# Two attentions on one Trainium2 core: a third buffer for transposed weights, halved GpSimd passes, a second raw weight slot

## The chip, the cores and the metric

The kernel runs on one core of a Trainium2 chip. The metric is the device time of one execution in microseconds. Three runs of the kernel before took 3191.88, 3189.90 and 3182.48 us (median 3189.9).

## What is computed

Two blocks follow each other on one sequence of 1024 tokens with 1024 channels, in float32. The first has a gated chunk mixer and an attention over 16 heads of 64 channels; the second has a state-space mixer, a per-layer embedding, a second attention of the "stick-breaking" kind, and another embedding. The two attentions, cut to what matters here:

```
# first attention (three dilations, here one table of added penalties)
q, k, v = heads(h @ w_in)                 # 16 heads x 1024 x 64
p = softmax(q k^T / 8 + alibi, causal)    # rows of weights, 128 at a time
y = (p v) * silu(h @ w_gate)
...
# second attention
q, k, v = norm(u @ s_in), norm(h @ w_kv), h @ w_kv'
z = q k^T;  w = sigmoid(z) * running product of sigmoid(-z) from the right
y = ((w v) * silu(gate)) @ w_out
```

Each matrix of weights is scaled by a row of gains where the reference has a norm in front of it, as in all projections of the second attention.

## The kernel before

Nothing here is scheduled by hand on the chip. The builder holds generators ("streams") with priorities and runs them against a small model of the engines (`Sched`, L207 on): whichever stream of highest priority is ready by the model emits its next instructions. What comes out is one fixed order for each engine, and each engine works through its own order and waits on semaphores. So a change of a buffer count changes the order in which everything near it is emitted.

Products are made in float32r as three matmuls, hi x hi, hi x lo and lo x hi. A weight block of 128x1024 elements is loaded from memory into a raw slot (`Weights.loads`, L384), multiplied on POOL (GpSimd) by its gain if it has one, copied as hi by ACT and subtracted as lo by POOL (`Weights.splits`, L397), which puts hi and lo into a split slot. There are two split slots in the attentions (`limit`, L434). Raw slots lie at 0, 4 and 208 KB of each partition; the first attention uses all three, the second only the one at 0, since 4 KB is used for other tiles there.

An attention goes over 8 pairs of heads. For each pair, `project_pair` makes v, q, k and the gate (12 or 24 matmuls of 512 columns in a row; low priority, so it fills what the attention leaves). The scores stream (`sstream`, L1403 and L2010) makes rows of scores: two matmuls of up to 512 columns for each PSUM bank of three (two in the first attention), then DVE, ACT and, in the second attention, a DVE scan (L2058) and a POOL product (through L521) turn a row into weights. `weigh` (L1283) has two streams on top: `xs` (L1292) transposes weights on PE in groups of up to four 128x128 blocks into one of two PSUM banks, ACT writes hi and DVE writes lo into a buffer of the resource `pt2`, and `vs` (L1321) multiplies that buffer with v, four matmuls a group, and releases it. `pt2` has two buffers of 4 KB, at 164 and 168 KB (L1390, L1997). There are 160 such groups in each attention. v of a pair lies in one of two slots, so v of pair p+1 can only be projected when the products of pair p-1 are done.

Names in the rows: psum<-ident,m172f is a transpose of weights; psum<-m156r,m140r or psum<-m156r with 256 columns or less is the product with v; psum<-m108r followed by psum<-m140r,m108r or m200r,m108r are scores; psum<-m44r,m8r and the like (m44r, m60r, m76r, m92r with m8r, m16r) are projections. L536 is every matmul, L547 every transpose, L521 every two-input POOL operation, L502 and L507 DVE, L498 most of ACT. After the second attention `stick_out` (L2161) multiplies its result, which goes through memory and POOL (`load_halves`, L2213), with the last projection matrix.

Of the kernel before, what the change touches and what calls it, by code (L numbers as in the profile page):

```python
# [15 lines left out]
ALU = mybir.AluOpType  # L16
# [6 lines left out]
P = 128  # L23
# [9 lines left out]
def R(ap):  # L33
    return ap.bitcast(F32R)
# [7 lines left out]
class Tok:  # L42


    def __init__(self, t=None):
        self.t = t
# [23 lines left out]
class Arena:  # L70


    CUTS = (0, 8, 16, 24, 40, 44, 60, 76, 92, 108, 140, 156, 172, 192, 200, 208, 216)

    def __init__(self, pool):
        self.pool = pool
        self.kb = [0.0] * self.CUTS[-1]
        self.blocks = [Block(a, b - a) for a, b in zip(self.CUTS, self.CUTS[1:])]
        self.of = [x for x in self.blocks for _ in range(x.n)]
# [286 lines left out]
class Weights:  # L366
# [30 lines left out]
    def splits(self):  # L397
        b = self.b
        for g in self.list:
            yield (g.loaded, self.split)  # L400
            g.out = self.split.get()
            n = g.nk * g.nc
            hi = g.out[:, :n].rearrange("p (k c) -> p k c", k=g.nk)
            lo = g.out[:, KB4:KB4 + n].rearrange("p (k c) -> p k c", k=g.nk)
            dep = g.loaded.t
            if g.gain is not None and g.nk <= 2:

                yield (dep, b.s.FA)
                for k in range(g.nk):
                    e = b.A(R(hi[:, k, :]), g.rawv[:, k, :], AF.Copy, dep, scale=g.gain[:, k:k + 1])  # L410
                for k in range(g.nk):
                    yield (e, b.s.FV)
                    t = b.Vstt(R(lo[:, k, :]), g.rawv[:, k, :], g.gain[:, k:k + 1], hi[:, k, :], ALU.mult, ALU.subtract, e)
                self.raw.put(g.slot, t)
                g.hi, g.lo = R(hi), R(lo)
                g.ready.t = t
                yield 0.0
                continue
            if g.gain is not None:
                yield b.s.FG  # L420
                dep = b.Gtt(g.rawv, g.rawv, g.gain.unsqueeze(2).to_broadcast([P, g.nk, g.nc]), ALU.mult, dep)
            if b.hi_on_pool:
                dep = b.Gts(R(hi), g.rawv, 1.0, 0.0, ALU.mult, ALU.add, dep)
            else:
                yield (dep, b.s.FA)
                dep = b.A(R(hi), g.rawv, AF.Copy, dep)
            yield (dep, b.s.FG)
            t = b.Gtt(R(lo), g.rawv, hi, ALU.subtract, dep)
            self.raw.put(g.slot, t)
            g.hi, g.lo = R(hi), R(lo)  # L430
            g.ready.t = t
            yield 0.0

    def limit(self, n, m=3):  # L434

        self.split.slots, self.raw.slots = self.all[:n], self.all_raw[:m]
# [5 lines left out]
class Builder:  # L442
    def __init__(self, ctx, tc, a, out=None):
        self.ctx, self.tc, self.nc, self.a, self.out = ctx, tc, tc.nc, a, out
        self.s = Sched()
        self.hi_on_pool = False
        nc = self.nc
        pool = lambda n, **k: ctx.enter_context(tc.tile_pool(name=n, bufs=1, **k))
        cp = pool("const")
        self.dram = pool("dram", space=DRAM)  # L450
        self.ident = cp.tile([P, P], F32, name="ident")
        make_identity(nc, self.ident)
        self.mhalf = cp.tile([P, 8], F32, name="mhalf")
        nc.gpsimd.memset(self.mhalf, -0.5)
        self.cols = cp.tile([P, 256], F32, name="cols")
        self.smallt = cp.tile([P, 256], F32, name="smalls")
        self.mask = cp.tile([P, P], F32, name="mask")
        nc.gpsimd.memset(self.mask, 0.0)
        nc.gpsimd.affine_select(self.mask, self.mask, pattern=[[-1, P]], compare_op=ALU.is_gt, fill=-1e30, base=0,
                                channel_multiplier=1)  # L460
        self.zero = cp.tile([P, 1], F32, name="zero")
        nc.gpsimd.memset(self.zero, 0.0)
        self.nsmall = 0
        self.rq = cp.tile([P, 96], F32, name="rq")
        self.ps = pool("psum", space=PSUM).tile([P, 8, 512], F32, name="psum")
        self.arena = Arena(pool("arena"))
        self.bank = [Bank(self.ps[:, i, :]) for i in range(8)]
        self.pg, self.pt, self.px, self.pv = [Res([]) for _ in range(4)]
# [574 lines left out]

    def merge(self):
        self.banks("012", "3", "456", "7")

        a, s = self.a, self.s
        gl, ml, ls = self.res(172, 4, 2), self.res(180, 4, 2), self.res(188, 4, 3)
# [43 lines left out]
        g = gr.get().rearrange("p (a c) -> p a c", a=2)  # L1092
# [289 lines left out]
    def attention1(self):  # L1382
# [4 lines left out]
        self.att_tok = self.halves()  # L1387
        self.stack_pools()
        pr = Ring(self, 172, 20)
        pt2, ops = self.res(164, 4, 2, "r"), self.res(192, 1, 2)  # L1390
        tmp, Ts = Res([self.region(o, 2) for o in (40, 42, 194, 196, 198)]), self.res(24, 4, 2)
        self.W.limit(2)
        self.new_pairs()

        T = {(p, h): Tok() for p in range(8) for h in range(2)}
# [593 lines left out]
    def stick(self):  # L1989
# [4 lines left out]
        self.stk_tok, self.sgd_tok = self.halves(), [Tok() for _ in range(8)]  # L1994
        self.stack_pools()
        pr, tr_ = Ring(self, 172, 20), Ring(self, 24, 16)
        pt2, ops = self.res(164, 4, 2, "r"), self.res(192, 1, 2)  # L1997
        tmp = Res([self.region(o, 2) for o in (4, 6, 40, 42, 194, 196, 198)])
        self.W.limit(2, 1)
        self.tail_slots, self.all_scored = tmp, Tok()  # L2000
        gains = self.smallt[:, 252:254]
        for o in (0, 64):
            e = self.dma(gains[o:o + 64, 0:1], a["q_norm_2"].rearrange("o d -> d o"))
            e = self.dma(gains[o:o + 64, 1:2], a["k_norm_2"].unsqueeze(1))
# [156 lines left out]
    def stick_out(self):  # L2161
        self.banks("012", "34", "567", "7")
        a, s = self.a, self.s
        act = self.act1
        W = self.W
        act.tt = self.next_tt

        def more():
            yield self.all_scored
            self.hi_on_pool = False  # L2170
            W.raw.slots = W.all_raw
            W.split.slots = W.all[:4] + [self.region(o, 8, "r") for o in (140, 148)]

        s.spawn(1, more())
        self.hq = self.scratch("hq", [S, D])
        ev0, begin0, hq_tok = self.partial(self.hq, self.tail_slots)

        turn = [Tok() for _ in range(NT)]

        def begin_turn(cb, t):  # L2180
            yield from begin0(cb, t)
            n = cb * NT + t - self.TURN[0]
            if n % self.TURN[1] == 0 and 0 <= n // self.TURN[1] < NT:
                turn[n // self.TURN[1]].t = s.now

        hd1 = [(self.all_scored, t, n) for t, n in zip(self.hd1_tok, turn)]
        hq_go = [(self.all_scored, t) for t in hq_tok]
        h, he, ha, hr = self.residual(self.res(108, 4, NT).slots, [(self.hd1, hd1), (self.hq, hq_go)], self.res(180, 4, 2))
        yield from self.gemm_a(act, self.J["so", 0], ev0, begin=begin_turn)
        nj, es, half = self.res(172, 4, 2), Res([self.region(o, 2) for o in (188, 190, 212, 214)]), {}  # L2190
        pact = self.embed(1, 156, self.res(188, 1, 4), self.weighed)

        def ev(cb, t, ps, e):
            sl = slice(cb * 512, cb * 512 + 512)
            return self.Vtt(h[t][:, sl], h[t][:, sl], ps, ALU.add, max(e, he[t].t))

        def fin(t, e):
            act.tt[0][t], act.tt[1][t] = Tok(), Tok()
            s.spawn(1, self.raw_tile(act, h[t], t, (e, ha[t]), nj, half))

        def begin(cb, t):
            yield he[t]

        yield from self.gemm_a(act, self.J["so", 1], ev, fin, 4, begin, (5, 6, 7))
        W.split.slots = W.split.slots + W.all[4:]

        def store(t, e):
            yield e
            self.dma(self.out[0, t * P:(t + 1) * P, :], h[t], e)

        yield from self.ple(1, act, pact, h, half, es, lambda t, e: s.spawn(1, store(t, e)))
# [70 lines left out]
```

## Time and profile before

| what | value |
|---|---|
| profiled execution | 3192.31 us, of which the span is 3190.6 us |
| median of three runs | 3189.9 us |
| TensorE busy | 3066.8 us, 96% of the span |
| VectorE, ScalarE, GpSimd busy | 1694.9, 1410.7 and 1104.3 us |
| mean granted TensorE clock | 0.978 of full speed |
| first attention | about 450 to 1040 us |
| second attention | about 2340 to 3020 us |

The time around the span is 1.7 us. TensorE (PE) is the engine with work nearly all the time, so the places to look at are those where it sits idle or where its granted clock falls below 1.00. The rows come from a view of busy time by stretches, from timelines of one engine, and from a table of who waited for whom.

### The profile page before, as it was taken

How to read it: one execution, taken by the hardware profiler on the slowest of the kernel's cores; microseconds unless marked ns; L12 is line 12 of the kernel's file. 1: busy time of each engine (PE TensorE's matmuls, PEld its weight loads, DVE VectorE, ACT ScalarE, POOL GpSimd, SP SyncE). 2: the span in 40 equal slices, each digit the busy share in tenths (PEclk: the TensorE clock that was granted, in tenths of full speed). 3: DMA queues.
4: the chain of work that ended last, by engine and by line, in shares of the span. 5: the costliest groups of instructions: out<-in, count | busy, mean ns of one | idle time of the engine just before them, and what ended most of it. 6: DMA issues, size and time to landing. Idle time of an engine off the chain costs nothing. (4 is left out here: it accounts for less than half of the span.)

```text
span 3190.6 us, 40526 instructions
## 1 busy us (share of the span) xinstructions
PE 3066.8 (96%) x15374; PEld 2557.1 (80%) x15374; DVE 1694.9 (53%) x3008; ACT 1410.7 (44%) x2511; POOL 1104.3 (35%) x694
## 2 busy tenths in 40 slices
PE   7999999999999999999999999999999999998899
PEld 6888888888888788888787877778887878887787
DVE  2111146666664422447676666463447777877552
ACT  4322145555564311324242424232457776776431
POOL 3323211111111333324455542401336655668510
PEclk9999999999999999999999999999999999999999
DMA  4112221221212754232333344470201111113621
GB/s 140 58 62 76 96 64 45 63 62 58 60 54 73 253 184 171 92 96 69 89 110 94 108 95 144 135 251 27 93 16 34 40 40 40 40 41 118 220 83 53
DMA packets 270551, 290.87 MB, mean 91 GB/s; under 512 B 14660, under 2 KB 202228, under 8 KB 270356
## 3 DMA queue, kind: packets, MB, share of 16 engines
q1 hardware_dynamic: 270356, 288.29, 28.9%
q8 instruction: 120, 1.97, 0.3%
q14 instruction: 75, 0.61, 0.1%
HBM read 216.80 MB, written 71.43 MB: 90 GB/s over the span
## 5 line engine op out<-in xcount | busy, mean ns | idle before, releaser
L502 DVE TENSOR_TENSOR m156r<-psum,m156r 128x384 fp32r<-128x384 f32 (+2 forms) x376 | 223.9, 605 | 147.6 <-ACT m156r L498 145.3
L498 ACT ACTIVATE m156r<-psum 128x384 fp32r<-128x384 f32 (+2 forms) x376 | 196.7, 535 | 185.6 <-PE psum L547 176.4
L521 POOL TENSOR_TENSOR m172f<-m172f,m24f 128x127 f32<-128x127 f32 (+7 forms) x128 | 181.0, 1424 | 156.2 <-DVE m24f L2058 108.2
L2058 DVE TENSOR_TENSOR_SCAN m24f<-m24f,zero 128x128 f32<-128x128 f32 (+7 forms) x128 | 219.4, 1722 | 6.5 <-ACT m24f L498 5.5
L547 PE MATMUL psum<-ident,m172f 128*128 128x128 f32 (+1 forms) x1314 | 206.5, 281 | 15.5 <-DVE m172f L507 7.2
L521 POOL TENSOR_TENSOR m16r<-m0f,m16r 128x1024 fp32r<-128x1024 f32 (+1 forms) x44 | 107.9, 2452 | 301.1 <-ACT m16r L498 250.3
L498 ACT ACTIVATE m192f<-psum 64x256 f32<-64x256 f32 (+2 forms) x230 | 102.1, 445 | 239.7 <-PE psum L536 137.7
L521 POOL TENSOR_TENSOR m8r<-m0f,m8r 128x1024 fp32r<-128x1024 f32 x42 | 102.7, 2445 | 274.9 <-ACT m8r L498 237.1
L547 PEld LDWEIGHTS psum<-ident,m172f 128*128 128x128 f32 (+1 forms) x1314 | 158.9, 144 | 43.8 <-DVE m172f L507 9.0
L521 POOL TENSOR_TENSOR smalls<-smalls,mhalf 128x1 f32<-128x1 f32 (+1 forms) x104 | 92.1, 886 | 278.4 <-DVE smalls L509 277.7
L536 PE MATMUL psum<-m108r 128*128 128x512 f32 (+3 forms) x384 | 143.2, 375 | 13.0 <-ACT m172f L498 11.3
L536 PE MATMUL psum<-m200r,m108r 128*128 128x512 f32 (+1 forms) x480 | 151.0, 395 | 0.0
L513 DVE SCALAR_TENSOR_TENSOR m172f<-m172f,psum 128x512 f32<-128x512 f32 x64 | 43.7, 686 | 188.9 <-ACT m172f L498 144.1
L1427 DVE CUSTOM_DVE_ANT_0 m172f<-psum,m24f 128x512 f32<-128x512 f32 (+1 forms) x192 | 102.8, 553 | 65.0 <-PE psum L536 64.8
L1435 ACT ACTIVATE m172f<-m172f,smalls 128x128 f32<-128x128 f32 (+7 forms) x128 | 99.3, 776 | 82.9 <-DVE smalls L509 81.2
L536 PE MATMUL psum<-m44r,m8r 128*128 128x512 f32 x504 | 134.6, 405 | 1.1 <-DVE m108r L513 1.1
L507 DVE TENSOR_SCALAR m172f<-m172f,smalls 128x512 f32<-128x512 f32 (+7 forms) x160 | 122.6, 766 | 24.3 <-POOL smalls L521 19.8
L536 PE MATMUL psum<-m60r,m8r 128*128 128x512 f32 x504 | 133.3, 398 | 0.3
L536 PE MATMUL psum<-m76r,m8r 128*128 128x512 f32 x504 | 132.3, 397 | 0.0
L536 PE MATMUL psum<-m60r,m16r 128*128 128x512 f32 x492 | 132.2, 399 | 0.0
L536 PE MATMUL psum<-m92r,m8r 128*128 128x512 f32 x504 | 130.7, 395 | 0.0
L536 PE MATMUL psum<-m44r,m16r 128*128 128x512 f32 x492 | 130.6, 402 | 0.0
(425 smaller groups left out, 7647.2 us busy)
## 6 DMA issues: line engine op xcount, KB each, us to landing
m0f<-in_w_in_dram SPq DMA_DIRECT2D x48, 512.0 KB, 3.8
m0f<-in_m_in_dram SPq DMA_DIRECT2D x26, 512.0 KB, 4.1
m208f<-in_w_in_dram SPq DMA_DIRECT2D x24, 512.0 KB, 3.8
m92f<-acum SPq DMA_DIRECT2D x21, 512.0 KB, 9.4
m24f<-in_alibi_dram SPq DMA_DIRECT2D x16, 512.0 KB, 4.6
m172f<-zd SPq DMA_DIRECT2D x32, 256.0 KB, 10.2
yd<-m172f SPq DMA_DIRECT2D x32, 256.0 KB, 2.3
m108f<-hd SPq DMA_DIRECT2D x16, 512.0 KB, 8.4
```

The lines of the kernel that those rows point to most:

```text
L498: self.nc.scalar.activation(out, in_, func, **k)
L502: self.nc.vector.tensor_tensor(out, a, b, op=op)
L507: self.nc.vector.tensor_scalar(out, a, s1, None, op0=op0)
L513: self.nc.vector.scalar_tensor_tensor(out, a, s, b, op0=op0, op1=op1)
L521: self.nc.gpsimd.tensor_tensor(out, a, b, op=op)
L536: self.nc.tensor.matmul(out, l, r, start=start, stop=stop)
L547: self.nc.tensor.transpose(out, in_, self.ident[:in_.shape[0], :in_.shape[0]])
L1427: nc.vector.tensor_tensor_reduce(row[:, k0:k0 + w], bank[:, :w], Tt[:, off + k0:off + k0 + w], 1.0, -3e38, op0=ALU.add, op1=ALU.max, accum ...
L1435: nc.scalar.activation(row[:, :n], row[:, :n], AF.Exp, bias=nm, accum_out=l)
L2058: nc.vector.tensor_tensor_scan(x[:, ::-1], x[:, ::-1], self.zero.to_broadcast([P, n]), 1.0, op0=ALU.mult, op1=ALU.add)
```

## The change

It does three things. `pt2` gets a third buffer of 4 KB at 212 KB in both attentions; for that the block of 8 KB at 208 is cut into two. While `short` is set, which is during the first attention and in the second up to the end of its scores, POOL's gain pass and its lo pass over a weight block of 128x1024 become two of 128x512 each. And the second attention has raw slots at 0 and 208 KB in place of the one at 0.

```diff
-    CUTS = (0, 8, 16, 24, 40, 44, 60, 76, 92, 108, 140, 156, 172, 192, 200, 208, 216)
+    CUTS = (0, 8, 16, 24, 40, 44, 60, 76, 92, 108, 140, 156, 172, 192, 200, 208, 212, 216)
...
             if g.gain is not None:
                 yield b.s.FG
-                dep = b.Gtt(g.rawv, g.rawv, g.gain.unsqueeze(2).to_broadcast([P, g.nk, g.nc]), ALU.mult, dep)
+                for ks in self.pieces(g):
+                    e = b.Gtt(g.rawv[:, ks, :], g.rawv[:, ks, :], g.gain[:, ks].unsqueeze(2).to_broadcast(
+                        [P, ks.stop - ks.start, g.nc]), ALU.mult, dep)
+                    yield b.s.FG
+                dep = e
...
-            t = b.Gtt(R(lo), g.rawv, hi, ALU.subtract, dep)
+            for ks in self.pieces(g):
+                t = b.Gtt(R(lo[:, ks, :]), g.rawv[:, ks, :], hi[:, ks, :], ALU.subtract, dep)
+                yield b.s.FG
...
+    def pieces(self, g):
+
+        n = g.nk // 2 if self.b.short and g.nk > 1 else g.nk
+        return [slice(k, min(k + n, g.nk)) for k in range(0, g.nk, n)]
...
-        pt2, ops = self.res(164, 4, 2, "r"), self.res(192, 1, 2)
+        pt2, ops = Res([self.region(o, 4, "r") for o in (164, 168, 212)]), self.res(192, 1, 2)
...
-        self.W.limit(2, 1)
+        self.W.limit(2)
+        self.W.raw.slots = [self.W.all_raw[0], self.W.all_raw[2]]
+        self.short = True
...
         def more():
             yield self.all_scored
+            self.short = False
```

The number of matmuls and transposes is the same, 14956. By kind of work the order on PE is the same outside the two attentions; what moves in the other stages is which PSUM bank or slot is taken. Of the 160 groups of transposed weights in each attention, 54 now go into the buffer at 212 KB (m212r). In POOL's order 88 passes are in halves, 30 in the first attention and 58 in the second, and the two halves always follow each other directly.

**First attention, PE, where pair 0 ends and pair 1 begins** (the row ahead of both pieces is the 256-column scores of pair 1; L536 and L547 are L547 and L558 in the changed file). Before:

```order
L536 MATMUL psum<-m92r,m8r 128x512 x3
L536 MATMUL psum<-m108r 128x384
L536 MATMUL psum<-m140r,m108r 128x384
L536 MATMUL psum<-m108r 128x512
L536 MATMUL psum<-m140r,m108r 128x512
L536 MATMUL psum<-m156r,m140r 128x256 x4
L547 MATMUL psum<-ident,m172f 128x128 x3
L536 MATMUL psum<-m156r,m140r 128x256 x4
L547 MATMUL psum<-ident,m172f 128x128 x3
L536 MATMUL psum<-m156r,m140r 128x256 x2
L536 MATMUL psum<-m156r,m140r 128x128 x2
L547 MATMUL psum<-ident,m172f 128x128 x4
```

Now:

```order
L547 MATMUL psum<-m92r,m8r 128x512 x3
L547 MATMUL psum<-m108r 128x384
L547 MATMUL psum<-m140r,m108r 128x384
L547 MATMUL psum<-m92r,m8r 128x512 x3
L547 MATMUL psum<-m156r,m140r 128x256 x4
L547 MATMUL psum<-m108r 128x512
L547 MATMUL psum<-m140r,m108r 128x512
L547 MATMUL psum<-m212r,m140r 128x256 x4
L547 MATMUL psum<-m156r,m140r 128x256 x2
L547 MATMUL psum<-m156r,m140r 128x128 x2
L547 MATMUL psum<-m44r,m16r 128x512 x9
L558 MATMUL psum<-ident,m172f 128x128 x3
```

Pair 0's last groups were transposed earlier, one of them into m212r, so their products stand together, and nine projection matmuls now stand between them and pair 1's first transposes.

**Second attention, PE, where pair 4 ends**, from one point of the work on. Before:

```order
L547 MATMUL psum<-ident,m172f 128x128 x4
L536 MATMUL psum<-m156r,m140r 128x256 x4
L547 MATMUL psum<-ident,m172f 128x128 x3
L536 MATMUL psum<-m108r 128x128
L536 MATMUL psum<-m140r,m108r 128x128
L536 MATMUL psum<-m108r 128x256
L536 MATMUL psum<-m140r,m108r 128x256
L536 MATMUL psum<-m156r,m140r 128x256 x6
L536 MATMUL psum<-m156r,m140r 128x128 x2
L547 MATMUL psum<-ident,m172f 128x128 x4
L536 MATMUL psum<-m108r 128x384
L536 MATMUL psum<-m140r,m108r 128x384
```

Now:

```order
L547 MATMUL psum<-m212r,m140r 128x256 x2
L547 MATMUL psum<-m212r,m140r 128x128 x2
L547 MATMUL psum<-m108r 128x128
L547 MATMUL psum<-m140r,m108r 128x128
L547 MATMUL psum<-m108r 128x256
L547 MATMUL psum<-m140r,m108r 128x256
L547 MATMUL psum<-m108r 128x384
L547 MATMUL psum<-m140r,m108r 128x384
L547 MATMUL psum<-m108r 128x512
L547 MATMUL psum<-m140r,m108r 128x512
L558 MATMUL psum<-ident,m172f 128x128 x8
L547 MATMUL psum<-m108r 128x512
```

The scores of four rows now stand back to back, where transposes and products stood between them.

**End of the second attention, PE** (m140r,m76r is the first product of the last projection that needs the last heads' results). Before:

```order
L536 MATMUL psum<-m156r 128x256 x8
L547 MATMUL psum<-ident,m172f 128x128 x3
L536 MATMUL psum<-m156r 128x256 x2
L536 MATMUL psum<-m156r 128x128 x2
L536 MATMUL psum<-m140r,m76r 128x512 x30
L547 MATMUL psum<-ident,m172f 128x128 x4
```

Now:

```order
L547 MATMUL psum<-m16r,m44r 128x512 x3
L547 MATMUL psum<-m212r,m156r 128x256 x2
L547 MATMUL psum<-m212r,m156r 128x128 x2
L547 MATMUL psum<-m16r,m44r 128x512 x3
L547 MATMUL psum<-m8r,m60r 128x512 x6
L547 MATMUL psum<-m16r,m60r 128x512 x6
L547 MATMUL psum<-m8r,m60r 128x512 x6
L547 MATMUL psum<-m16r,m60r 128x512 x6
L547 MATMUL psum<-m8r,m60r 128x512 x6
L547 MATMUL psum<-m16r,m60r 128x512 x6
L547 MATMUL psum<-m8r,m60r 128x512 x6
L547 MATMUL psum<-m16r,m60r 128x512 x6
L547 MATMUL psum<-m140r,m76r 128x512 x48
```

The last product with v now has 51 projection matmuls behind it before m140r,m76r begins, where it stood in the midst of those.

## Rows read from the trace of the kernel before

**Rows 1.** Profile page, part 1, and busy time of the two attention stages (us, each engine's busy us, PEclk, DMA share).

```profile
PE 3066.8 (96%) x15374; PEld 2557.1 (80%) x15374; DVE 1694.9 (53%) x3008; ACT 1410.7 (44%) x2511; POOL 1104.3 (35%) x694
...
455.00:1030.00 575.00, 563.58 (x3099) 485.33 (x3097) 376.66 (x1041) 331.55 (x664) 77.12 (x32) 0.99 0.20 60
2340.00:2960.00 620.00, 585.08 (x3170) 492.37 (x3169) 468.78 (x650) 432.80 (x821) 378.07 (x227) 0.96 0.16 47
```

**Rows 2.** Busy time in three stretches of the first attention, same columns.

```profile
500.00:520.00 20.00, 16.43 (x93) 13.60 (x93) 14.38 (x34) 13.02 (x28) 2.34 (x1) 0.83 0.14 37
660.00:680.00 20.00, 16.75 (x78) 14.09 (x77) 12.40 (x34) 10.78 (x21) 2.26 (x1) 0.83 0.14 39
800.00:820.00 20.00, 16.74 (x99) 14.57 (x98) 13.81 (x36) 13.00 (x28) 2.36 (x1) 0.91 0.13 37
```

**Rows 3.** PE timeline of the first attention (start, us, instruction, idle before).

```profile
513.22 0.41 PE L547 MATMUL psum<-ident,m172f 128*128 128x128 f32 x1 [2.09 <-DVE m172f L507]
514.53 0.69 PE L547 MATMUL psum<-ident,m172f 128*128 128x128 f32 x2 [0.91 <-DVE m172f L507]
```

**Rows 4.** PE timeline of an undisturbed stretch of the second attention.

```profile
2464.68 0.64 PE L536 MATMUL psum<-m156r 128*128 128x256 f32 x4
2465.15 0.60 PE L547 MATMUL psum<-ident,m172f 128*128 128x128 f32 x4
2465.50 2.32 PE L536 MATMUL psum<-m92r,m8r 128*128 128x512 f32 x9
2467.66 0.62 PE L536 MATMUL psum<-m44r,m16r 128*128 128x512 f32 x2
```

**Rows 5.** Busy time in the nine stretches of the second attention that lose.

```profile
2420.00:2460.00 40.00, 32.32 (x165) 26.26 (x165) 36.10 (x48) 30.63 (x62) 25.89 (x16) 0.87 0.11 30
2500.00:2540.00 40.00, 37.65 (x208) 31.66 (x208) 27.10 (x41) 30.51 (x56) 19.51 (x12) 0.96 0.16 48
2580.00:2640.00 60.00, 54.21 (x289) 45.36 (x288) 39.55 (x57) 41.25 (x79) 31.28 (x21) 0.91 0.12 35
2680.00:2700.00 20.00, 16.22 (x75) 13.15 (x74) 13.58 (x20) 14.85 (x27) 5.64 (x6) 0.83 0.17 50
2760.00:2800.00 40.00, 38.12 (x207) 31.27 (x206) 32.41 (x48) 30.95 (x63) 26.11 (x17) 0.96 0.11 32
2840.00:2860.00 20.00, 18.08 (x90) 14.70 (x89) 16.20 (x23) 16.26 (x31) 7.16 (x6) 0.91 0.19 58
2920.00:2960.00 40.00, 30.39 (x150) 23.79 (x149) 34.87 (x36) 21.97 (x44) 34.30 (x27) 0.91 0.47 155
2960.00:3000.00 40.00, 34.99 (x185) 29.12 (x185) 22.64 (x31) 23.31 (x47) 22.90 (x15) 0.96 0.34 114
3000.00:3040.00 40.00, 34.62 (x166) 27.42 (x165) 21.65 (x31) 13.98 (x27) 20.05 (x14) 0.91 0.95 354
```

**Rows 6.** PE's waits from 2340 to 2960 us (total, times, longest).

```profile
PE psum L536 <- ACT m172f L498: 11.3, 10, 1.9
...
PE psum L547 <- POOL m172f L521: 4.7, 4, 2.8
```

**Rows 7.** PE timeline at the end of the second attention.

```profile
2972.03 0.74 PE L536 MATMUL psum<-m8r,m44r 128*128 128x512 f32 x2 [1.86 <-POOL m8r L521]
...
2980.99 1.09 PE L536 MATMUL psum<-m16r,m44r 128*128 128x512 f32 x2 [2.80 <-POOL m16r L521]
...
3020.27 9.54 PE L536 MATMUL psum<-m140r,m76r 128*128 128x512 f32 x30 [2.94 <-POOL m76r L525]
```

**Rows 8.** POOL groups by form, 2340 to 2920 us (count, busy us, mean ns, idle before).

```profile
L521 POOL TENSOR_TENSOR m16r<-m0f,m16r 128x1024 fp32r<-128x1024 f32 x13 | 32.2, 2480 | 26.2 <-ACT m16r L498 26.2
...
L521 POOL TENSOR_TENSOR m192f<-m192f,m0f 128x512 f32<-128x512 f32 x1 | 1.3, 1307 | 0.0
```

**Rows 9.** POOL and DVE timelines of one moment of the second attention.

```profile
2426.88 2.36 POOL L521 TENSOR_TENSOR m16r<-m0f,m16r 128x1024 fp32r<-128x1024 f32 x1
...
2428.08 2.51 DVE L2058 TENSOR_TENSOR_SCAN m24f<-m24f,zero 128x640 f32<-128x640 f32 x1 [1.06 <-ACT m24f L498]
```

## What the change will do to the time

> **What bounds the kernel now.** I read the page first: PE is busy 96% of the span [rows 1], so time can only come from where PE sits idle or runs at the lower of its two levels (1.2 in place of 2.4 GHz). Then busy time by stages: in the first attention PE idles 575 - 563.6 = 11.4 us, in the second 620 - 585.1 = 34.9 us at a mean clock of 0.96 [rows 1]. Then stretches of 20 us, to see where. The loss of a stretch I count as its idle time plus (1 - PEclk) x its length; the second part is what the lower clock takes from matmuls that had work.
>
> In the first attention three stretches hold nearly everything [rows 2]: idle 3.6 + 3.3 + 3.3 = 10.1 us, and (0.17 + 0.17 + 0.09) x 20 = 8.6 us of clock, in sum **18.7 us**. The timeline shows what happens there [rows 3]: a transpose waits 2.09 us for DVE's scaling of a row of weights (L507), and the next but one 0.91 us. POOL works 2.3 of 20 us in these stretches, so no weight block is late; the chain from scores to weights is, at the change of pairs 0/1, 2/3 and 4/5.
>
> The second attention loses in nine stretches [rows 5]: 12.9, 4.0, 11.2, 7.2, 3.5, 3.7, 13.2, 6.6 and 9.0 us, in sum **71 us**, 43 of it idle and 28 clock. PE waits there above all for ACT to read score banks, 11.3 us, and 4.7 us for POOL's products [rows 6]; DVE works 36.1 of 40 us in the first of the nine and POOL 34.3 of 40 in the seventh, so these stretches are bound by more than one engine. At the end PE waits 1.86 and 2.80 us for weight blocks and 2.94 us for the last heads' result [rows 7].
>
> **First attention.** What counts for a wait is how much PE work the order puts between the cause and the one that waits. I price it at the pitch of an undisturbed stretch [rows 4]: four 256-column matmuls 0.47 us, four transposes 0.35, nine 512-column ones 2.16, so 0.24 each; others in proportion. Before, between pair 1's 256-column scores and the transposes of that row lie the rows that the first pieces of order show, 2.7 us; the next unit has 1.9 us. The waits of 2.09 and 0.91 us [rows 3] came on top, so the chain needs about 4.8 us. Now the same two distances are 5.6 and 4.6 us, because the third buffer let pair 0's last groups be transposed early and nine projection matmuls come first. The distances at pairs 3 and 5 change in the same way; the even pairs have 5.6 and 4.4 us already, and all other stretches of the stage together idle 11.4 - 10.1 = 1.3 us. So the three stalls go, but for some 0.5 us each: **-17 us**. Bounds: -10 if only the idle time comes back and the low clock stays or falls elsewhere, -19 if all does.
>
> **Second attention.** I did the same for all 160 groups. Of the nine places, the second, fourth and sixth (4.0, 7.2 and 3.7 us) no longer have a product with v less than 2 us behind its transposes, and the third has one where it had three; the third buffer again. Three stay or get worse. At the first (12.9 us) no projection was left to fill with for 13 us of PE work, and that is still so; and a score bank is now reused within 1.5 us of PE work 11 times in the stage where it was 6 times, mostly here: I put 15. At the fifth (3.5 us) the second pieces of order show four rows' scores back to back: 9. At the seventh (13.2 us) the same, and one transpose comes 1.3 us after its row's last scores: 16. The eighth is helped by the second raw slot: the load of the next block of the last projection no longer waits for POOL to finish the block before, which is part of the 1.86 and 2.80 us [rows 7]: 4. In the ninth the 2.94 us wait goes, since 51 projection matmuls, 51 x 0.24 = 12 us, now stand between the last product and the first matmul that needs it (third pieces of order), but four of the last products stand only 0.4 to 0.7 us behind their transposes: 8. Third place: 5. Sum 15 + 0 + 5 + 0 + 9 + 0 + 16 + 4 + 8 = 57 against 71, so -14. The distances explained the stalls before only in part (the third place lost twice what they say), so half of the 15 us that I cancel in the second, fourth and sixth place I put back: **-7 us**. Bounds: -23 if those vanish and the others stay as they were, +5 if new stalls of their size come elsewhere.
>
> **Halved passes.** One pass of 128x1024 takes 2.36 us when nothing holds it [rows 9], 2.48 in the mean, and 128x512 took 1.31 [rows 8]. Two halves are 2.61, so 58 passes in the second attention add 58 x 0.25 = 15 us to POOL's 378 of 620 us. The halves follow each other directly in POOL's order, so nothing gets in between and no other POOL instruction starts earlier. What hides the 15 us is that POOL is 61% busy there; at the seventh place that cover is gone, and my 16 us include it. In the first attention POOL is busy 77 of 575 us: nothing.
>
> There is one more effect. A DVE scan of 640 columns that began 1.2 us into a POOL pass took 2.51 us and ended 1.35 us after the pass did [rows 9], as if it had begun only then. That is how the Trainium skill tells it (SBUF — State Buffer, "Who interferes with whom"): a DVE instruction with two SBUF inputs and a GpSimd instruction that reads SBUF hold a shared port pair one after the other, each for its whole length. The trace agrees at this moment. By that rule the longest hold of a weight pass falls from 2.4 to 1.3 us; with one such meeting at each of seven pair changes that is at most 7 x 1.1 = 8 us, and the sum would be 3160. No row shows a half pass that meets a scan, so my sum has 0 for it.
>
> **Loads.** The 27 weight blocks of the second attention now alternate between two raw slots, so each load is issued earlier. PE's waits for blocks in the stage are those of rows 7, at its end, and SP carries the same number of transfers: 0, but for the end, which is counted above.
>
> **Sum.** 3192.3 us (the profiled execution: span 3190.6 and 1.7 around it) - 17 - 7 = **3168 us**. The median of the runs is 3189.9, 2.4 lower; 0.3% of it, about what a measurement can tell from no change, is 9.6 us, so faster means below 3180.3 and slower above 3199.5.
>
> **Rivals.**
> - *Both attentions give.* The stalls at all pair changes of the second attention go, not only those that the distances show: -19 - 23 = -42, 3150 us. For it speaks that each stall avoided also avoids a low clock; against it, DVE at 36 of 40 us in the first place. Chance 0.16.
> - *The second attention takes back what the first gives.* Transposes that run ahead spend DVE and ACT time at the pair changes, scores come in bursts, and banks wait for ACT, which already makes up 11.3 us [rows 6]. If that doubles, and the low clock with it, +10 against -17: 3185 us, no change that can be told. Chance 0.16.
> - *Slower: POOL at the pair changes.* Rows' products (L521, m172f) stand in POOL's queue behind the halves, and the distance from a row's last scores to its transposes in the second attention falls from 17.0 to 11.3 us in the median of the 64 units, so less late work on POOL is forgiven. It decides once POOL is some 10 us behind at a pair change; the wait then is what four cost before, up to 2.8 us each [rows 6]. Two of these at each of seven pair changes are 39 us: 3192 - 17 + 39 = 3214 us. By the rule of the Trainium skill named above each further POOL start can also be held by a scan; that would make it likelier. Against it: POOL at 25.9 of 40 us in the first place [rows 5]. Chance 0.06.
> - *The third buffer is not used.* Excluded by the order: 54 groups of 160 in each attention use it.
>
> **How the numbers follow.** The forecast, 3155 to 3180 us, has 0.62, with the better case 0.16: faster 0.78. Same 0.16, slower 0.06. The range goes from -42 (3150) to first attention -10 and second +5 (3187): it leaves out the slower case, half of the no-change case and a little of the better one.
>
> **What would show it.** In the profile after: in the first attention no wait of PE for DVE m172f L507 above 0.5 us, and no stretch with a clock of 0.83. In the second, fewer stretches with a low clock but the first, fifth and seventh not better; waits for ACT m172f of 15 us or more; POOL busy some 390 us in its 620; no wait for POOL m76r of 2.9 us at the end. I am wrong if the three stalls of the first attention stay, if the second attention as a whole gets longer, or if waits for POOL m172f pass 15 us.

## The result and the profile after

The change takes **3151.2 us** (median of four runs, 3149.5 to 3154.7); the kernel before took 3187.2 beside it. The ratio is 0.9889, 95% interval 0.9873 to 0.9905: 36 us less. The forecast was 3168, with 3150 to 3187 as its range. The profiled execution took 3151.55 us, its span 3149.8.

Part 1 of the page of the change, then its busy time in the two attentions and in a stretch behind the first (columns as in [rows 1]):

```profile
PE 3037.4 (96%) x15374; PEld 2539.1 (81%) x15374; DVE 1680.7 (53%) x3008; ACT 1412.5 (45%) x2511; POOL 1126.4 (36%) x783
...
455.00:1030.00 575.00, 574.80 (x3208) 495.24 (x3207) 378.84 (x1052) 344.00 (x681) 90.36 (x62) 1.00 0.21 63
1040.00:1100.00 60.00, 58.49 (x256) 47.46 (x255) 21.00 (x27) 17.70 (x29) 26.26 (x11) 1.00 0.85 277
2340.00:2960.00 620.00, 577.26 (x3186) 489.97 (x3184) 467.07 (x659) 440.12 (x840) 408.95 (x289) 0.96 0.18 53
```

PE's 11.4 us of idle time in the first attention became 0.2, at a clock of 1.00. The second attention did not get quieter: 585.1 us of PE work in its 620 before [rows 1], 577.3 now. The stretch from 1040 to 1100 us, for which nothing was forecast, had before:

```profile
1040.00:1100.00 60.00, 54.56 (x236) 43.42 (x235) 24.79 (x29) 24.99 (x40) 24.21 (x10) 0.91 0.72 233
```

The loss as the prediction counts it (idle time plus what the lower clock takes), from stretches of 20 us by sections of the program, one profile each; the last columns come from experiments told of below:

| section | before | change | slot in first only | slot in second only | whole passes | halves, other order (two profiles) |
|---|---|---|---|---|---|---|
| ahead, to 440 us | 16.3 | 16.2 | 16.7 | 16.9 | 16.8 | 18.1, 17.0 |
| first attention, to 1030 | 20.0 | 0.2 | 4.6 | 18.7 | 4.6 | 0.2, 0.2 |
| behind it, to 1200 | 10.6 | 1.5 | 0.3 | 10.2 | 0.6 | 0.7, 0.6 |
| state-space mixer, to some 2240 | 65.5 | 59.9 | 66.0 | 73.0 | 58.3 | 62.2, 56.9 |
| second attention and its end | 74.9 | 72.2 | 81.6 | 58.9 | 63.9 | 58.2, 56.6 |

By this measure the change gains 19.8 us in the first attention, 9.1 behind it, 5.6 in the mixer and 2.7 in the second attention. The mixer's part belongs to no edit: kernels that run the same order in it lost 53.9 to 73.0 us there. The 2.7 us can't be told from nothing either: two kernels of the experiments below that keep the order of before in the second attention, with whole passes, lost 68.8 and 71.2 us there. The measure is rough, too: between two profiles told of below, of the change and of the version with halves in the other order, it differs by 22.7 us and the spans by 12.6.

At the first change of pairs PE's timeline now reads, where [rows 3] had waits of 2.09 and 0.91 us:

```profile
510.98 2.29 PE L547 MATMUL psum<-m44r,m16r 128*128 128x512 f32 x9
513.11 0.66 PE L558 MATMUL psum<-ident,m172f 128*128 128x128 f32 x3
```

And PE's waits in the second attention, 2340 to 2960 us, the rows that answer to [rows 6]:

```profile
PE psum L547 <- ACT m172f L509: 13.8, 12, 4.5
PE psum L558 <- POOL m172f L532: 7.1, 4, 2.8
```

### The profile page after: what moved, and what is told of

The parts are those of the page before. It is cut to its first block, busy times and chain, and to the rows that moved or that the text cites. A ratio compares the mean times of both kernels' runs of the same rounds, so it can differ in the third digit from the quotient of the medians.

```text
span 3149.8 us, 40650 instructions
## 1 busy us (share of the span) xinstructions
PE 3037.4 (96%) x15374; PEld 2539.1 (81%) x15374; DVE 1680.7 (53%) x3008; ACT 1412.5 (45%) x2511; POOL 1126.4 (36%) x783
## 4 chain that ended last, share of the span: by engine, by line
PE 47%; DVE 6%; DMA 5%; POOL 4%; issue 3%; ACT 1%; SPq 0%; POOLq 0%; DVEq 0%; ACTq 0%
PE psum L547 43%; PE psum L558 4%; DMA m92f<-acum 2%; DVE m24f L2073 1%; DVE m44f L524 1%; POOL m172f L532 1%; DMA m172f<-acum 1%; DVE m172f L513 0%; DMA m172f<-zd 0%; POOL m8r L532 0%; DVE m92f L520 0%; DMA m44f<-yd 0%; POOL m208f L532 0%; POOL m16r L532 0%; POOL smalls L532 0%
## 5 line engine op out<-in xcount | busy, mean ns | idle before, releaser
L532 POOL TENSOR_TENSOR m16r<-m0f,m16r 128x512 fp32r<-128x512 f32 (+1 forms) x70 | 118.8, 1712 | 314.7 <-ACT m16r L509 287.0
L532 POOL TENSOR_TENSOR m172f<-m172f,m24f 128x127 f32<-128x127 f32 (+7 forms) x128 | 172.7, 1358 | 138.1 <-DVE m24f L2073 108.5
L558 PE MATMUL psum<-ident,m172f 128*128 128x128 f32 (+1 forms) x1314 | 207.8, 279 | 11.4 <-POOL m172f L532 8.3
L513 DVE TENSOR_TENSOR m156r<-psum,m156r 128x512 fp32r<-128x512 f32 (+2 forms) x268 | 158.3, 596 | 90.8 <-ACT m156r L509 89.4
L509 ACT ACTIVATE m156r<-psum 128x512 fp32r<-128x512 f32 (+2 forms) x268 | 140.1, 528 | 132.4 <-PE psum L558 126.6
L558 PEld LDWEIGHTS psum<-ident,m172f 128*128 128x128 f32 (+1 forms) x1314 | 156.5, 143 | 37.4 <-POOL m172f L532 11.7
L547 PE MATMUL psum<-m108r 128*128 128x512 f32 (+3 forms) x384 | 142.6, 375 | 14.8 <-ACT m172f L509 13.8
L532 POOL TENSOR_TENSOR m8r<-m0f,m8r 128x512 fp32r<-128x512 f32 (+2 forms) x38 | 72.3, 1914 | 235.9 <-ACT m8r L509 235.9
L532 POOL TENSOR_TENSOR m8r<-m208f,m8r 128x512 fp32r<-128x512 f32 (+1 forms) x50 | 85.2, 1720 | 137.2 <-ACT m8r L509 137.0
L547 PE MATMUL psum<-m60r,m8r 128*128 128x512 f32 x480 | 127.6, 400 | 5.0 <-DVE m108r L524 5.0
L532 POOL TENSOR_TENSOR m24r<-m0f,m24r 128x1024 fp32r<-128x1024 f32 x33 | 82.1, 2489 | 138.5 <-ACT m24r L509 135.6
L547 PE MATMUL psum<-m60r,m16r 128*128 128x512 f32 x492 | 130.8, 399 | 0.0
L547 PE MATMUL psum<-m24r,m108r 128*128 128x512 f32 (+1 forms) x504 | 130.2, 393 | 0.0
L547 PE MATMUL psum<-m44r,m16r 128*128 128x512 f32 x492 | 130.0, 397 | 0.0
L547 PE MATMUL psum<-m200r,m108r 128*128 128x512 f32 (+2 forms) x480 | 130.0, 356 | 0.0
L547 PE MATMUL psum<-m92r,m16r 128*128 128x512 f32 x492 | 129.4, 397 | 0.0
```

Source lines behind the costliest of these rows:

```text
L509: self.nc.scalar.activation(out, in_, func, **k)
L513: self.nc.vector.tensor_tensor(out, a, b, op=op)
L532: self.nc.gpsimd.tensor_tensor(out, a, b, op=op)
L547: self.nc.tensor.matmul(out, l, r, start=start, stop=stop)
L558: self.nc.tensor.transpose(out, in_, self.ident[:in_.shape[0], :in_.shape[0]])
```

## The experiments

What the prediction had not read shows in two rows of the kernel before at the first stall, a POOL pass over a weight block and DVE's scaling of a row (start, us):

```profile
510.74 2.34 POOL L521 TENSOR_TENSOR m8r<-m208f,m8r 128x1024 fp32r<-128x1024 f32 x1 [19.78 <-PE psum L547]
```

```profile
511.08 2.08 DVE L507 TENSOR_SCALAR m172f<-m172f,smalls 128x128 f32<-128x128 f32 x1
...
514.12 0.35 DVE L507 TENSOR_SCALAR m172f<-m172f,smalls 128x256 f32<-128x256 f32 x1
```

The scaling of 128 columns took 2.08 us where that of 256 took 0.35, and it ended 0.08 us after the pass did (513.16 and 513.08). This is no single meeting: in the timelines of the whole first attention all 12 scalings of rows that began with or inside a POOL pass ended 0.08 to 0.56 us after it, and the three that began up to 0.35 us ahead of a pass took their usual 0.42 to 0.62 us. The theory from here on: the pass holds DVE's scaling; the halves shorten that hold, and the new order takes the row out of its way. The rival was the prediction's own account, the distance in the order alone.

**Third slot in the first attention only**, passes whole, the second attention with two buffers:

```diff
 def attention1(self):
-        pt2, ops = self.res(164, 4, 2, "r"), self.res(192, 1, 2)
+        pt2, ops = Res([self.region(o, 4, "r") for o in (164, 168, 212)]), self.res(192, 1, 2)
```

> The third buffer for transposed weights in the first attention alone, nothing else. Theory (the order does it: projection matmuls now stand between the pairs, and the attention ends earlier against the projections): the first attention loses under 1 us where it lost 20.0 (idle 11.4 and clock 8.6), the 60 us behind it lose 1 to 3 us where they lost 10.6, the second attention stays at about 75; in sum -26 to -34 us, some 3157 us. Rival (the halved passes, by the shared port, are part of the gain in the first attention): the three stalls shrink but do not go, -8 to -15 us. Second rival (the stage behind the first attention gained by chance or by the halves): first attention 0.2, stage behind still 8 to 11, -20 us.

3172.8 us, ratio 0.9957 (0.9941 to 0.9973), where the theory had some 3157. The first attention keeps 4.6 us of loss of 20.0, so the stalls shrink but do not go, as the first rival has it, and the section behind it 0.3 of 10.6. Of the 26 us that these two give, 7 go back in the second attention, whose code is as before but which the scheduler emitted in another order.

**Third slot with the order held**: the buffer exists, but the scheduler may run ahead only as far as two allow.

```diff
-                    yield (self.w_tok[u], self.pt, pt2)
+                    yield (self.w_tok[u], self.pt, Some(pt2, 2))
```

> Three buffers in both attentions, used in turn, but a group is begun only when two of the three are free, so at most two are in use and all five engines keep the order of the kernel before. Theory (the gain is what the order puts between the pairs, not the buffer): the three stalls of about 3.3 us in the first attention stay, loss of the stage 18 to 21 us, time within 5 us of the kernel before. Rival (a wait for the buffer itself, of ACT's write behind the last product, was what held the chain, or where the buffers lie matters): the stalls shrink by half or more, -10 us or better.

3188.9 us, ratio 1.0008 (0.9995 to 1.0020); the first attention lost 18.5 us, and PE's waits for the scaling stayed, before and in this run:

```profile
PE psum L547 <- DVE m172f L507: 7.2, 4, 2.1
```

```profile
PE psum L547 <- DVE m172f L507: 7.3, 4, 2.1
```

A free buffer alone gives nothing. What the slot gives comes from the order that it permits.

**Halves with the order held**: the two pieces are issued where the one pass stood; every engine but POOL has the instructions of before in their order.

```diff
+    def Ghalf(self, out, a, b, op, dep=0.0):
+        n = out.shape[1] // 2
+        for k in (slice(0, n), slice(n, 2 * n)):
+            self.nc.gpsimd.tensor_tensor(out[:, k, :], a[:, k, :], b[:, k, :], op=op)
+        return self.s.op("G", 150 + 2.1 * out.free_size(), dep)
```

> The kernel before with POOL's gain and lo passes in two halves issued together, all else in the old order. Theory (a half costs a fixed part more and nothing else starts earlier): POOL busy 10 to 16 us more in the second attention, time within 5 us of the kernel before. Rival A (shared port: a DVE scan is held by 1.3 us at most in place of 2.4): the mean scan of 640 columns falls from 1.96 us to under 1.8 and that of 1024 from 2.70 to under 2.55, the second attention loses 5 to 10 us less. Rival B (POOL falls behind at the pair changes): PE's waits for POOL m172f, 4.7 us before, pass 10 us, time 5 to 15 us longer.

3176.9 us, ratio 0.9967 (0.9953 to 0.9982): halves give 11 us with no change of order, where the theory had nothing that can be told. The first attention lost 15.2 us, against 18.5 to 20.1 in the kernels with its old order and whole passes; that is 3 to 5 us of the 11. Where the rest lies isn't shown: the second attention lost 66.8 us in this one profile. The signs of rival A did not come (scans of 640 and 1024 columns 2.01 and 2.68 us in the mean), nor that of rival B (waits for POOL's products 8.2 us). At the first stall the scaling now took:

```profile
510.01 2.49 POOL L528 TENSOR_TENSOR m8r<-m208f,m8r 128x512 fp32r<-128x512 f32 x2 [19.63 <-ACT m8r L499]
```

```profile
510.36 1.00 DVE L508 TENSOR_SCALAR m172f<-m172f,smalls 128x128 f32<-128x128 f32 x1
```

It ended with the first half, not with the second. At the changes 2/3 and 4/5 PE still waited 2.24 us; there the second half held the scaling, which took 1.37 and 1.38 us and ended 0.08 and 0.07 us after the pass.

**The change with whole passes**: third slot in both attentions and second raw slot.

```diff
-        n = g.nk // 2 if self.b.short and g.nk > 1 else g.nk
+        n = g.nk
```

> The changed kernel with whole POOL passes (third buffer in both attentions and the second raw slot stay). Theory (the halves are worth nothing): first attention loses under 1 us, stage behind it 1 to 3 us, the second attention 65 to 80 us, in sum 3145 to 3160 us. Rival (the halves carry part of the gain): 3165 us or more, with the part that is missing lost in the second attention, where 58 of the 88 halved passes are.

3154.9 us, ratio 0.9898 (0.9883 to 0.9914), so some 3 us above the change by the ratios, within their intervals. In the first attention it has the 4.6 us of the first experiment again, where the theory had under 1. At the first change of pairs a whole pass holds the scaling of 256 columns, and PE waits for it:

```profile
511.14 2.38 POOL L532 TENSOR_TENSOR m8r<-m208f,m8r 128x1024 fp32r<-128x1024 f32 x1 [17.00 <-ACT m8r L509]
```

```profile
511.19 2.48 DVE L518 TENSOR_SCALAR m172f<-m172f,smalls 128x256 f32<-128x256 f32 x1
```

```profile
513.73 0.44 PE L558 MATMUL psum<-ident,m172f 128*128 128x128 f32 x2 [1.05 <-DVE m172f L518]
```

**Quarters with the order held**, as the halves above but with `n = m // 4`:

> The kernel before, with the same instructions in the same order on TensorE, VectorE, ScalarE and SyncE; only GpSimd's two passes over a weight block in both attentions are cut into four pieces that follow each other directly. Theory (a VectorE instruction that meets a GpSimd pass is held until that pass ends, and this hold is what the three stalls of the first attention are made of): in halves the scaling of the weights at the first change of pairs fell from 2.08 to 1.00 us; in quarters no scaling of 128 columns takes over 0.8 us, and the loss of the first attention (idle time and low clock) falls below the 15.2 us that halves left, to 6 to 13 us; in all 3165 to 3178 us. Rival 1 (the stalls are a matter of the order alone, and the gain with halves was chance): the first attention loses 15 to 20 us again, 3178 to 3190. Rival 2 (every further start costs GpSimd time that someone waits for): some 150 starts more at 0.06 to 0.1 us add 10 to 15 us to GpSimd in the second attention, and it loses more than the 67 us with halves; 3180 to 3195.

3184.2 us, ratio 0.9989 (0.9976 to 1.0002). The scalings at the first stall came down to 0.47, 0.47 and 0.69 us, and the first attention's loss to 12.1, as the theory had it. The total did not follow, and lies in the range of rival 2. That it is GpSimd's longer passes that take the gain back isn't shown: the second attention lost 71.4 us in this profile, 66.8 with halves, and 68.8 to 74.9 with whole passes in this order. Four starts cost POOL 2.83 us a pass, two 2.49, one 2.34:

```profile
510.97 2.83 POOL L529 TENSOR_TENSOR m8r<-m208f,m8r 128x256 fp32r<-128x256 f32 x4 [19.36 <-PE psum L555]
```

```profile
511.32 0.47 DVE L508 TENSOR_SCALAR m172f<-m172f,smalls 128x128 f32<-128x128 f32 x1
```

**Short rows scaled on ScalarE**, passes whole, order held:

```diff
         def norm(u, q, row, l, e):
+            if u[2] == 0:
+                nc.scalar.activation(row, row, AF.Copy, scale=l)
+                self.w_tok[u][q].t = s.op("V", 225 + 0.52 * row.free_size(), e)
+                return
```

> The kernel before, its order on TensorE, GpSimd and SyncE unchanged and its passes whole; in the first attention alone the scaling of the two shortest rows of weights of each unit (128 and 256 columns, 32 instructions) goes from VectorE to ScalarE. GpSimd's pass over the weight block stays where it was. Theory of the hold (a VectorE instruction from SBUF to SBUF waits for GpSimd's pass, a ScalarE one does not): the scaling takes some 0.4 us though it begins within the pass, TensorE's wait of 2.09 us for it at the first change of pairs goes, and the loss of the first attention falls from 20 to 12 us or less; what is left is other VectorE work that meets the passes. In all 3170 to 3184. Rival (the 2.08 us are the memory's, which any engine that reads these tiles would see): the scaling on ScalarE takes 2 us too, and the loss stays at 18 to 20. Rival (the chain of the row is late by the distance in the order alone, and the scaling only ends last): the scaling is short, but TensorE waits as long for it or for an instruction next to it; 18 to 20 again, 3184 to 3190.

3177.3 us, ratio 0.9971 (0.9959 to 0.9983), and 12.1 us of loss in the first attention. POOL, DVE and ACT at the first change of pairs:

```profile
510.82 2.36 POOL L521 TENSOR_TENSOR m8r<-m208f,m8r 128x1024 fp32r<-128x1024 f32 x1 [19.78 <-PE psum L547]
```

```profile
511.05 0.67 DVE L1427 CUSTOM_DVE_ANT_0 m172f<-psum,m24f 128x512 f32<-128x512 f32 x1
...
512.14 1.25 DVE L507 TENSOR_SCALAR m172f<-m172f,smalls 128x384 f32<-128x384 f32 x1
```

```profile
511.71 0.39 ACT L1447 ACTIVATE m172f<-m172f,smalls 128x128 f32<-128x128 f32 x1
```

Inside the same pass, ACT's scaling of the row took 0.39 us and DVE's operation with a PSUM input 0.67; DVE's next scaling from SBUF to SBUF began at 512.14 and ended at 513.39, 0.21 us after the pass. This is the clearest of the runs: it is neither the tile nor its memory, but DVE's access from SBUF to SBUF beside POOL. It is what the Trainium skill says (SBUF — State Buffer, "Who interferes with whom"): beside operations with two SBUF inputs, which the prediction named, that section lists tensor-scalar operations among those that can enter a mode with two ports and then contend with GpSimd, and it has ScalarE wait for nobody. The runs agree in both (1.25 us for DVE's scaling, 0.39 for ACT's); which mode the scaling ran in no profile says. PE's wait of 2.09 us became 0.93. At the changes 2/3 and 4/5 it still was 1.90 and 1.89, there because ACT's scaling stood behind an exponential of 512 columns. So a part of the stalls is a chain that is late without a hold of the short rows: here, as with quarters, 12.1 of some 20 us are left.

**Third slot in the second attention only**: the `pt2` line in that function, one raw slot, whole passes.

> The kernel before with the third slot in the second attention alone, whole passes, one raw slot there. Theory: the first attention and the stage behind it stay as they were (20 and 11 us lost); the second attention, by itself, gives 0 to 10 us: 3177 to 3190. Rival (the second attention gives as much as the first): 65 us lost or less there in place of 75, and under 3175. Rival (it takes back): 3195 or more.

3172.8 us, ratio 0.9949 (0.9930 to 0.9968). The rival of that text held: the slot gives 14 us there by itself, and the loss fell from 74.9 to 58.9.

**Second raw slot only**:

```diff
-        self.W.limit(2, 1)
+        self.W.limit(2)
+        self.W.raw.slots = [self.W.all_raw[0], self.W.all_raw[2]]
```

> The kernel before with the second raw weight slot of the second attention alone. Theory: nothing that can be told, within 8 us of the kernel before (loads are not late there; at the end 0 to 4 us of the waits for weight blocks go). Rival (the loads that no longer wait for GpSimd count): 8 to 15 us less, with shorter waits for m8r and m16r in the last 250 us.

3187.8 us, ratio 0.9996 (0.9985 to 1.0008): nothing that can be told. At the end it moved a wait without shortening the time: PE's wait for m16r fell from 2.80 us [rows 7] to 0.42, and that for m76r grew from 2.94 to 5.22.

**Halves in the order of the kernel with whole passes** (all three parts of the change, the two pieces issued together, so that the scheduler's order is that of the experiment with whole passes), twice, and the same in quarters:

> The order of e4_no_halves held on every engine (third slot, second raw slot), with the passes cut in two at the place where each one stood. Theory of the hold: what e4 lost in the first attention (4.6 us, six waits of up to 1.1 us for the scaling of the weights) falls below 1 us, as in the change; the total is 0 to 4 us under e4, 3148 to 3155. Rival (the whole change owed its undisturbed first attention to the order that its halves led to): the 4.6 us stay. Rival (GpSimd's extra time is paid at the changes of pairs of the second attention): 3155 to 3165.

> As e10, the passes in four pieces. Theory: the first attention as with halves; in the second each hold is shorter again by up to 0.6 us, and GpSimd busier by 10 to 15 us: within 4 us of e10. Rival of the price: 5 to 15 us slower than e10 by longer waits of TensorE for the products of GpSimd in the second attention.

> The kernel of e10_halves_in_e4_order once more. Theory (the pauses that the change's code puts between the two pieces lead the build's scheduler to an order of the second attention that loses some 10 us more): 4 to 8 us under the change of the same call, and the second attention loses 58 to 65 us against 70 to 74. Rival (the 6 us between them are the difference of two calls): within 3 us of it.

> The change itself once more, on the same chip and in the same rounds as the kernel with halves in the other order. 3148 to 3155 us, 0.987 to 0.990 of the kernel before.

Halves: 3145.3 us, ratio 0.9872 (0.9857 to 0.9887), and measured again 3141.1, 0.9855 (0.9841 to 0.9870). Quarters: 3147.3, 0.9880 (0.9866 to 0.9895), no better. The change itself, measured beside the 3141.1: 3152.5, 0.9887 (0.9871 to 0.9902). The version with the other order is **11 us faster than the change**, more than the 4 to 8 that were expected. Against the kernel before beside each, it takes 41 and 47 us less, and whole passes in the same order 33: the halves give 9 to 15 us there, more than the 0 to 4 expected. The first attention is as quiet (0.2 us), so the halves, not some further shift of the order, took the last 4.4 us there. What the version gains over the change lies in the second attention. Three stretches of it, of the change and then of this version (the 3141.1):

```profile
2380.00:2420.00 40.00, 27.85 (x131) 22.02 (x129) 30.99 (x38) 29.74 (x57) 17.21 (x13) 0.74 0.11 34
2720.00:2760.00 40.00, 34.79 (x185) 28.39 (x186) 32.20 (x47) 31.47 (x64) 25.79 (x19) 0.91 0.09 27
2880.00:2920.00 40.00, 28.47 (x131) 22.26 (x130) 36.60 (x40) 21.22 (x44) 37.08 (x29) 0.83 0.47 150
```

```profile
2380.00:2420.00 40.00, 30.97 (x157) 25.55 (x156) 32.25 (x44) 34.86 (x67) 18.56 (x13) 0.83 0.09 27
2720.00:2760.00 40.00, 38.38 (x217) 32.84 (x218) 30.63 (x49) 30.27 (x61) 23.74 (x16) 1.00 0.08 22
2880.00:2920.00 40.00, 32.54 (x161) 26.67 (x162) 33.28 (x40) 21.99 (x45) 29.90 (x25) 0.91 0.36 117
```

PE waits less for ACT to read score banks, 2.9 us where the change had 13.8; with whole passes in this order it was 3.3, so that is the order's doing:

```profile
PE psum L553 <- ACT m172f L509: 2.9, 4, 1.2
```

So the form in which the change issues its pieces costs 5 to 11 us of the 9 to 15 that they gain: it moves the scheduler to an order with bursts of scores. Two things differ in that form, and they were not tried apart: a pause behind each piece (`yield b.s.FG` in the loop over `pieces`) in place of one behind the pass, and the 150 ns that the scheduler's model books for the start of the second piece, which `Ghalf` does not book. That the bursts are what costs was argued from the waits for score banks, not tried by itself.

## Why the prediction was right, and where it was not

**First attention: right in size, with half of the reason.** -17 was forecast and -19.8 measured; no wait of PE for the scaling is left, and no stretch below clock 1.00. That the order and not the buffer does it was right too: with the order held nothing was gained. But the step "the chain needs about 4.8 us" took the scaling as part of a chain of fixed length. 1.8 of its 2.08 us were the hold (undisturbed, at 510.64 us of the change, it took 0.29), and at the changes 2/3 and 4/5 0.95 of 1.24. The new order alone, with whole passes, leaves 4.6 us; the halves took these.

**Halved passes: the step that failed.** "In the first attention POOL is busy 77 of 575 us: nothing" judged an engine by its share. Its one pass of 2.34 us in the stretch of 20 covered the scaling of 2.08 us that PE was waiting for. In a held order the halves gave 11 us, and in the order of the whole passes 9 to 15; 3 to 5 us of either lie in the first attention, and how the rest comes about is open. The change as it stands shows only some 3 of it, since its pieces also moved the order. The sum by the Trainium skill's rule, at most 8 us, came nearer to what the halves do in a held order than the 0 that stood in the sum. The hold was looked for at the pair changes of the second attention, where only the scan was read; it was shown in the first. In the second the scans got shorter with the order held, the short ones most; before and with halves:

```profile
L2058 DVE TENSOR_TENSOR_SCAN m24f<-m24f,zero 128x256 f32<-128x256 f32 x14 | 18.4, 1311 | 0.1
```

```profile
L2068 DVE TENSOR_TENSOR_SCAN m24f<-m24f,zero 128x256 f32<-128x256 f32 x15 | 16.3, 1087 | 0.1
```

By the means from 2340 to 2920 us, fourteen scans of each of the eight sizes come to 191 us before, 186 with halves and 179 with quarters in the same order. What of that PE gains is not shown.

POOL's own price was as forecast: 1126.4 - 1104.3 = 22 us for 89 instructions more (783 against 694), 0.25 us each. The trace has 59 passes in halves in the second attention, one more than the 58 of the forecast. PE's waits for POOL's products in the stage rose from 4.7 us [rows 6] to 7.1.

**Second attention: the places right, the remainder a little optimistic.** -7 was forecast, -2.7 measured (and about 0 in the second profile of the change, which lost 75.7); neither can be told from nothing. By places, some 40 us earlier in the new span, forecast and measured: first 15 and 22.4, second 0 and 0, third 5 and 1.2, fourth 0 and 0, fifth 9 and 8.6, sixth 0 and 0, seventh 16 and 18.3, eighth 4 and 4.8, ninth 8 and 3.7; in sum 57 and 59.0. Outside these places 4 us became 13; for that stood the 7 put back. So the distances told where the stalls go. What they did not tell is that this is one order of several: the slot alone led to one that loses 58.9. At the first place the waits for banks are the largest part, 4.8 of PE's 12.6 us of waits, and one wait of 2.83 us for POOL's product comes next; the longest for a bank came at the fifth:

```profile
2723.76 0.69 PE L547 MATMUL psum<-m108r 128*128 128x384 f32 x1 [4.46 <-ACT m172f L509]
```

At the end the wait of 2.94 us for m76r [rows 7] went, as forecast; that for m8r fell from 1.86 to 0.30 us, and that for m16r stayed with 2.69. With the second raw slot alone it was the one for m16r that fell, so the gain of the eighth place is not shown to be that slot's.

**Behind the first attention: not in the sum.** 9.1 us came from a section for which the order "by kind of work" was the same. PE waited there for tiles made of `ya`, 3.44 us and 1.75 us; the longer wait:

```profile
1081.89 1.95 PE L536 MATMUL psum<-m140r,m200r 128*128 128x512 f32 x3 [3.44 <-ACT m140r L498]
```

The loads of `ya`, before and after:

```profile
L529 SPq DMA_DIRECT2D m172f<-ya x3: 320/339/383, 1048.1 to 1065.7; - x3
```

```profile
L540 SPq DMA_DIRECT2D m172f<-ya x4: 319/320/383, 1024.3 to 1048.9; - x4
```

They start 24 us earlier, more than the 20 us that the stage before it became shorter, and in the first experiment, with 15 us less in that stage, 20 earlier (1028.1). The gain goes with the slot of the first attention alone and is absent with the order held (10.7 us). That the loads wait for space which the attention now frees earlier was argued, not tried. It may as well be a store that stands ahead of them in SP's order: SP issued the first load 0.4 us after `ga<-m192f` before (1047.67) and 1.6 us after it now (1022.77).

**The rivals.** The total came out at the time of the better case (3150), but not by it: the second attention did not give 23. What brought it there, past the forecast 3168, is the section behind the first attention and the 5.6 us of the mixer, so that nearness is luck. Nor did the second attention take back what the first gave: waits for banks rose from 11.3 to 13.8 us and did not double. Of the slower case only 2.4 us more of waits for POOL's products showed, where it priced 39.

## What to carry to other kernels

Before a wait is put down to the order, look at how long the instruction that ended it ran, beside its like: a DVE operation of 2.08 us among ones of 0.35 points to another engine's instruction that ended with it. Cutting a long GpSimd pass in two was worth most here where it changed nothing else, and four pieces gave no more; under a scheduler, first see what the order becomes, and try to issue the pieces as one step. An extra buffer is worth what the order does with it, and that is settled by the order that comes out, stage by stage, with the stage behind it.

## What the runs showed of the hardware that was not expected

A GpSimd pass of two SBUF inputs held a DVE scaling with one tensor input until it, or its first half, ended: the rows above show 2.08, 2.48, 1.25 and 1.00 us for work of 0.29 to 0.42. The time from the end of the pass to the end of the scaling grew with the row: 0.08 us for 128 columns, 0.35 for 640 and 0.55 for 1024 in the kernel before. A scaling that began ahead of the pass was not held. A DVE operation reading PSUM (0.67) and ACT's scaling (0.39) ran through the same kind of pass undelayed. And the lower clock differs between executions of one order: in the mixer, 1300 to 2200 us, PE worked nearly the same 858 us with a mean clock of 0.97 or 0.99 (slot in the second attention only, then short rows on ScalarE; both have the order of before there):

```profile
1300.00:2200.00 900.00, 858.19 (x4213) 702.19 (x4212) 544.41 (x854) 316.64 (x522) 337.25 (x245) 0.97 0.39 114
```

```profile
1300.00:2200.00 900.00, 858.42 (x4288) 704.29 (x4287) 550.37 (x859) 317.43 (x522) 337.40 (x244) 0.99 0.39 114
```

That is 0.02 x 900 = 18 us between two profiles, so a stage's difference of some 5 to 10 us of clock in single profiles shows nothing by itself; the ratios of the runs decide.
